# Four gate products behind the conformer, three steps of distance in the attention, and a projection tile behind each of ten chunks

## The chip, the cores and the metric

The kernel runs on one core of one Trainium2 chip. The metric is device microseconds of one execution, the median of several. The kernel before took 2198.22 us, the median of three runs from 2196.39 to 2204.89.

## The reference

Two layers of a hybrid trunk, over 1024 latent tokens and a context of 256, 1024 channels wide, in float32. The first layer adds a bidirectional state-space branch (SSD, 16 heads, chunks of 128 tokens: ten chunks with the context) and a conformer branch, whose result is multiplied by a gate; both go through one output projection. The second layer adds a gated chunk MLP and a windowed attention with sinks, again with one output projection.

```python
def even_mixer(h_x, h_c, w_in, ...):
    z_x, xbc_x, dt_x, glu_x, gate_x = _split(h_x @ w_in, EVEN_SIZES)
    ya_x, _, _ = ssd_branch(z_x, xbc_x, dt_x, hf_c, hb_c, ...)
    def merge(ya, glu, gate):
        yb = conformer_conv(glu, cv_w, cv_b, cv_ln_g, cv_ln_b) * jax.nn.silu(gate)
        return jnp.concatenate([ya, yb], axis=-1) @ w_out

def window_attention(q, k, v, k_ctx, v_ctx, sink):
    def block(args):
        s_lat = jnp.einsum('bqkrd,bskd->bkrqs', qblk, kblk) * ATT_SCALE
        s_lat = jnp.where(mblk, s_lat, -jnp.inf)
        s_ctx = jnp.einsum('bqkrd,bskd->bkrqs', qblk, k_ctx) * ATT_SCALE
        p = jax.nn.softmax(jnp.concatenate([s_lat, s_ctx, s_snk], axis=-1), axis=-1)
        return p[..., :3 * W] @ v_window + p[..., 3 * W:-1] @ v_ctx

def reference(x, c, ctx, c_ctx, ...):
    for layer in range(DEPTH):
        y_x, y_c = even_mixer(...) if layer % 2 == 0 else odd_mixer(...)
        x = layer_norm(DEEPNORM_ALPHA * x + g_x * y_x, ln_g[layer], ln_b[layer])
```

## The kernel before, in words

Every float32 product is made of three matmuls: each operand is split into a high part (a cast on ACT) and a low part (a subtraction on DVE or POOL), and high x high, low x high and high x low are summed in PSUM. So names come in pairs: hhi and hlo, wh and wl, zh and zl, yh and ylo, ph and pl.

**First layer, projections.** The input projection is computed channel by channel: 128 output channels over 1280 tokens in three slices (SLICES, two of 512 and one of 256 columns). The list `seq` sets the order of the GLU channels ("g"), the SSD channels ("x") and the early gates ("s"). An early gate's matmuls are followed by a SiLU on ACT and a store of the result to HBM (gs_d, L1277 and L1278), since its partner, the conformer's output cv, does not exist yet. After the list the conformer's layer norm is applied (it begins with the sums csum at L1324; its last scaling is L936 and L937), then z blocks 0 and 1 and early gate 2 are computed, then `dt_prep` (decays of the SSD on ACT and DVE, with small matmuls L1450 to L1492 and tables rA_d and rB_d stored at L1494), then `ssd_back`, the backward states of the ten chunks from the last to the first: each step loads a chunk (xtok, L1508), multiplies it on DVE (L1512), decays the state Hb on POOL (L1528), adds two bst matmuls (L1532, L1536) and stores the state to hb_d (L1523). z block 2 is computed beside it.

**Gates.** The loop at the end of `gates` takes the gates in the order 3, 0, 1, 4, 5, 6, 7, 2. `gate(i)` computes the first three with 75 matmuls each (L171) and multiplies the SiLU by cv[i] on POOL (L1393); for the five early ones it loads each slice of gs_d into one of four small tiles (tag "th"), multiplies it on POOL (L1386) and stores it to yb_d (L1387). Between them stand the loads of seven weight tiles wb of the output projection. yb_d is the input of the projection's second half.

**SSD stage and first output projection.** `stage_b(c)` is the part of the output projection that takes one chunk's 128 tokens of yb (48 matmuls at L1001; L159 splits its operands). It is written behind the SSD chunks: `S[c].prep`, `mix` and `finish` compute the forward states (tmp on POOL at L1567, two matmuls at L1574) and outputs. The order of instructions on each engine is set in this part of the program by the scheduler of the framework, which interleaves what is written; each engine then works in that order. SP issues nearly all DMAs, in order, and a DMA that waits holds those behind it.

**Attention.** It is the exception: the PE order is written by hand (L601). 16 units (4 key-value heads x 4 pairs of blocks) make 152 steps. A step computes the scores of one key block (L720, L721), takes the exponential (L723), splits it into ph (ACT, L730) and pl (POOL or DVE, L731), and LA steps later multiplies it with the values (L738). `att_max` is a generator that is advanced a few times in each step: it prepares the next unit's queries (mv, L664), makes score maxima (L678, L683), transposes the packed maxima (L705) and sends one row of them by POOL's DMA (L708) into the next unit's mv, which that unit's first L721 reads. `beside` fills each step with matmuls of `rest`: projections q and g, the opening of the second output projection ("W": gate rows by L222, weights wor loaded into the pool wr), its first half c (L1001) and its second half d (L832, with u from DVE at L842). What is left of `rest` when the last step is done runs as the tail.

```python
                LA = 2
                for n in range(len(seq) + LA):
...
                        fly.append(self.att_s(KV[kv % 2], mv[u], b, x, kb, off))
...
                now[0] = 99
                run(oth)
```

## Time and profile before

| | before |
|---|---|
| median of three runs | 2198.22 us |
| profiled execution | 2200.34 us, span 2198.6 us |
| PE matmul | 2054.9 us busy, 93% |
| DVE | 1348.8 us, 61% |
| ACT | 991.9 us, 45% |
| POOL | 979.8 us, 45% |
| mean granted clock of PE | 0.974 |
| chain that ended last | PE 64%, POOL 13%, DVE 9%, ACT 6%, DMA 5% |

Busy time of PE includes matmuls at a lower granted clock, so a stretch can be busy and still lose time. An engine other than PE matters where PE waits for it; the table of waits and the chain say where. The rows of single stages stand further below.

### The profile page before, as it was taken

Reading aid. Unit: us, or ns where it says so; the run is one execution under the profiler, and the core shown is the slowest. Engines: PE = TensorE matmul, PEld = TensorE weight load, DVE = VectorE, ACT = ScalarE, POOL = GpSimd, SP = SyncE. Lnnn points to the kernel's source line nnn. Section 1 sums busy time; section 2 is a strip of 40 time slices with the busy share of each in tenths; the row PEclk is TensorE's granted clock in tenths of the full one; section 3 lists DMA queues with packets and bytes.
Section 4 is the critical chain, followed back from the end, with each engine's and each line's share of the span. In section 5 each row is a group of like instructions: output and inputs, shape, how many; then the busy total and the mean of one; then the engine's idle time right before and its main releaser. Section 6 shows DMA issues by size and latency. Waiting matters only on the chain.

```text
span 2198.6 us, 28297 instructions
## 1 busy us (share of the span) xinstructions
PE 2054.9 (93%) x10636; PEld 1630.2 (74%) x10636; DVE 1348.8 (61%) x1889; ACT 991.9 (45%) x1549; POOL 979.8 (45%) x654
## 2 busy tenths in 40 slices
PE   7999999999979929999899999999999999899997
PEld 6888888889767716665488788888777676676675
DVE  6788896758445036667776321422566767676677
ACT  6455677533352122224234323233656767655510
POOL 0198999700112254546431113822445555434453
PEclk9999999999989969999899999999999999899998
DMA  8011122236637464464243422522311212534463
GB/s 306 30 39 39 51 79 85 96 129 213 218 106 250 169 221 149 146 214 157 98 159 125 134 70 82 179 99 80 99 49 51 59 52 57 159 92 126 122 182 130
DMA packets 158994, 269.33 MB, mean 123 GB/s; under 512 B 18901, under 2 KB 98385, under 8 KB 158601
## 3 DMA queue, kind: packets, MB, share of 16 engines
q1 hardware_dynamic: 157432, 264.01, 36.8%
q0 software_dynamic: 1280, 3.26, 0.5%
q8 instruction: 83, 1.36, 0.3%
q14 instruction: 55, 0.44, 0.1%
q10 hardware_dynamic: 144, 0.26, 0.0%
HBM read 189.82 MB, written 77.59 MB: 122 GB/s over the span
## 4 chain that ended last, share of the span: by engine, by line
PE 64%; POOL 13%; DVE 9%; ACT 6%; DMA 5%; issue 4%; SPq 0%; POOLq 0%; DVEq 0%; ACTq 0%
PE m L171 31%; PE m L1001 12%; POOL accq L1234 11%; PE po L738 3%; PE mz L1306 2%; PE po L1621 1%; PE m L832 1%; PE st L721 1%; PE st L720 1%; PE ms L208 1%; PE sg L1632 1%; ACT mv L664 1%; PE yd L1642 1%; ACT rb L425 1%; DVE wol L159 1%
## 5 line engine op out<-in xcount | busy, mean ns | idle before, releaser
L1234 POOL TENSOR_TENSOR accq<-accq,prod 128x1295 f32<-128x1295 f32 x90 | 287.7, 3197 | 33.9 <-ACT prod L1233 17.2
L171 PE MATMUL m<-hhi,wh 128*128 128x512 f32 (+1 forms) x792 | 280.9, 355 | 1.8 <-ACT th L1277 0.9
L171 PE MATMUL m<-hlo,wh 128*128 128x512 f32 (+1 forms) x792 | 280.6, 354 | 0.0
L171 PE MATMUL m<-hhi,wl 128*128 128x512 f32 (+1 forms) x792 | 280.2, 354 | 0.0
L1242 DVE SCALAR_TENSOR_TENSOR acc<-u,vwh,acc 128x1295 f32<-128x1295 f32 x150 | 235.2, 1568 | 12.9 <-ACT acc L1239 9.7
L731 POOL TENSOR_TENSOR pl<-pt,ph 128x512 fp32r<-128x512 f32 x96 | 130.1, 1356 | 198.9 <-ACT ph L730 195.9
L171 PE MATMUL m<-h1hi,wh 128*128 128x512 f32 (+1 forms) x544 | 213.3, 392 | 1.6 <-ACT rb L425 1.4
L171 PE MATMUL m<-h1lo,wh 128*128 128x512 f32 (+1 forms) x544 | 213.4, 392 | 0.0
L171 PE MATMUL m<-h1hi,wl 128*128 128x512 f32 (+1 forms) x544 | 212.3, 391 | 0.0
L1001 PE MATMUL m<-wol,yh 128*128 128x512 f32 x448 | 183.4, 409 | 4.6 <-DVE wol L954 2.5
L1001 PE MATMUL m<-woh,yh 128*128 128x512 f32 x448 | 185.9, 418 | 1.6 <-DVE t L1624 0.8
L1001 PE MATMUL m<-woh,ylo 128*128 128x512 f32 x448 | 181.6, 405 | 0.6 <-DVE ylo L159 0.6
L1233 ACT ACTIVATE prod<-u,vwh 128x1295 f32<-128x1295 f32 x90 | 124.1, 1382 | 97.9 <-POOL accq L1234 95.5
L171 PEld LDWEIGHTS m<-hhi,wh 128*128 128x128 f32 x792 | 149.7, 189 | 24.2 <-ACT th L1277 1.6
L171 PEld LDWEIGHTS m<-hhi,wl 128*128 128x128 f32 x792 | 149.7, 189 | 20.9
L171 PEld LDWEIGHTS m<-hlo,wh 128*128 128x128 f32 x792 | 149.8, 189 | 20.5
L730 ACT CAST ph<-pt 128x512 fp32r<-128x512 f32 x152 | 92.9, 619 | 97.6 <-PE po L738 86.2
L159 POOL TENSOR_TENSOR wl<-wr,wh 128x1024 fp32r<-128x1024 f32 x33 | 81.7, 2477 | 118.6 <-ACT wh L158 95.9
L738 PE MATMUL po<-ph,vs 128*66 128x512 f32 x304 | 121.6, 400 | 1.2 <-ACT ph L730 1.2
L171 PEld LDWEIGHTS m<-h1hi,wh 128*128 128x128 f32 x544 | 102.8, 189 | 22.6 <-ACT rb L425 2.0
L171 PEld LDWEIGHTS m<-h1hi,wl 128*128 128x128 f32 x544 | 102.9, 189 | 21.2
L171 PEld LDWEIGHTS m<-h1lo,wh 128*128 128x128 f32 x544 | 102.9, 189 | 19.9
(371 smaller groups left out, 4771.9 us busy)
## 6 DMA issues: line engine op xcount, KB each, us to landing
wr<-in_wch_dram SPq DMA_DIRECT2D x69, 512.0 KB
mw<-in_modw_dram SPq DMA_DIRECT2D x24, 512.0 KB
mr<-in_modw_dram SPq DMA_DIRECT2D x16, 512.0 KB
wor<-in_wout_dram SPq DMA_DIRECT2D x16, 512.0 KB
xbc_d<-acc SPq DMA_DIRECT2D x12, 640.0 KB
xcT<-xbc_d SPq DMA_DIRECT2D x20, 320.0 KB
xt_d<-xtok SPq DMA_DIRECT2D x20, 320.0 KB
xtok<-xt_d SPq DMA_DIRECT2D x10, 640.0 KB
```

The lines of the kernel that those rows point to most:

```text
L159: (nc.gpsimd if pool_lo else nc.vector).tensor_tensor(lo, src, hi.bitcast(F32), op=ALU.subtract)
L171: nc.tensor.matmul(out, x(k), y(k), start=(c == 0), stop=(c == tot - 1))
L208: nc.tensor.matmul(ps[:4, :P], self.scond[:, n * h + k], w[j][:, k], start=(h + j + k == 0), stop=(h + j + k == halves + n - 1))
L425: nc.scalar.copy(tb[d, :n], ps[s])
L730: nc.scalar.copy(ph, p)
L731: (nc.gpsimd if x in (0, 1, 3) else nc.vector).tensor_tensor(pl, p, ph.bitcast(F32), op=ALU.subtract)
L738: nc.tensor.matmul(po[:66], vs[:, kb, v], p[y], start=first and i == 0, stop=last and i == 2)
L1001: nc.tensor.matmul(ps[f], y[u][:, k], w[k][v][:, 512 * f:512 * f + 512], start=i + j == 0, stop=i + j == 9)
L1233: nc.scalar.activation(pr, u[:, k:k + N], AF.Copy, scale=vwh[:, i, k:k + 1])
L1234: nc.gpsimd.tensor_tensor(acc, acc, pr, op=ALU.add)
L1242: nc.vector.scalar_tensor_tensor(acc[:, :N], u[:, k:k + N], vwh[:, i, k:k + 1], acc[:, :N], op0=ALU.mult, op1=ALU.add)
L1306: nc.tensor.matmul(mz[0][32 * g:32 * g + 2, P * c:P * c + P], self.scond32[:, 2 * k:2 * k + 2], w[:, k], start=k == 0, stop=k == 7)
```

## The change

Four edits, made together.

- **Early products.** The gates 4 to 7 are still computed early. Directly behind the conformer, each of them is now loaded whole (128x1280) from gs_d into one tile gse (tag "accq", one buffer), multiplied by cv on POOL and stored to yb_d in three slices. Gate 2 is no longer an early gate: it is computed in the same place, but multiplied at once. The last loop holds the gates 3, 0 and 1 alone, with the weight loads in groups of three, two and two.
- **Projection tiles.** stage_b(2), with the operand y0, is written behind chunk 0 instead of ahead of the first chunk's prep, and a stage_b stands behind each of the ten chunks.
- **Attention.** LA is 3 instead of 2, ph and pl have three buffers instead of two, `att_max` yields four times instead of once behind mv, the opening of the second output projection (W) yields three times first, and the pool wr of its weights has two buffers instead of three, with two loaded ahead.
- **Tail.** The PSUM banks that the projection's halves take in turn are five instead of two once the last step of the attention is done.

```diff
--- before.py
+++ after.py
@@ -296,15 +296,13 @@
             self.mmt = ("m0", "m1")
             self.ko = (*range(1, 8), 0)
             S = [SsdFwd(self, c, xbc_d, xt_d, hb_d, zs_d, wt_d, rstd, q) for c in range(NT)]
-            self.stage_b(2, ob, w, yb_d, tb_d, grow, y0)
             S[0].prep()
             for c in range(NT):
                 S[c].mix()
                 if c < NT - 1:
                     S[c + 1].prep()
                 S[c].finish()
-                if c < NT - 1:
-                    self.stage_b((c + 3) % NT, ob, w, yb_d, tb_d, grow)
+                self.stage_b((c + 2) % NT, ob, w, yb_d, tb_d, grow, y0 if c == 0 else None)
                 if c == 7:
                     wl3 = ea.enter_context(self.pool(name="wl3", bufs=1))
                     for k in range(4, 6):
@@ -561,12 +559,14 @@
                         yield from (proj_q if n[0] == "q" else proj_g)(int(n[1]), int(n[2]))
                     elif n == "R":
                         self.er.close()
-                        wr = eq.enter_context(self.pool(name="wr", bufs=3))
+                        wr = eq.enter_context(self.pool(name="wr", bufs=2))
                         raws = []
-                        for k in range(3):
+                        for k in range(2):
                             raws.append(wr.tile([P, D], F32, name="wor", tag="wor"))
                             nc.sync.dma_start(raws[k], A["wout1"][k])
                     elif n == "W":
+                        for _ in range(3):
+                            yield None
                         ew.close()
                         free_h1()
                         out = self.out1_open(yc_d, wr, raws)
@@ -611,7 +611,7 @@
                 fly = []
                 mx = iter(())
                 acc = None
-                LA = 2
+                LA = 3
                 for n in range(len(seq) + LA):
                     if n < len(seq):
                         u, b, x, kb, off = seq[n]
@@ -647,6 +647,7 @@
                     beside(d * 0.2)
                     next(mx, None)
                 now[0] = 99
+                self.mmt = ("m0", "m1", "m2", "ms", "ms")
                 run(oth)
             eq.close()
 
@@ -665,7 +666,8 @@
                 nc.vector.tensor_tensor(mv2[0:64, :, 2 * i + hh], src,
                                         mv1[64 * hh:64 * hh + 64, :, 2 * i + hh].bitcast(F32), op=ALU.subtract)
         out[u] = mv1, mv2
-        yield
+        for _ in range(4):
+            yield
         pack_ = q.tile([P, 2, 2, 4], F32, name="mpack")
         mx = q.tile([P, 2, 2, 4], F32, name="mxs")
         for b in range(2):
@@ -725,8 +727,8 @@
 
             nc.gpsimd.affine_select(out=p, in_=p, pattern=[[0, 4], [off, P]], base=0, channel_multiplier=-off,
                                     compare_op=ALU.is_ge, fill=0.0)
-        ph = q.tile([P, 4, P], FR, name="ph", bufs=2)
-        pl = q.tile([P, 4, P], FR, name="pl", bufs=2)
+        ph = q.tile([P, 4, P], FR, name="ph", bufs=3)
+        pl = q.tile([P, 4, P], FR, name="pl", bufs=3)
         nc.scalar.copy(ph, p)
         (nc.gpsimd if x in (0, 1, 3) else nc.vector).tensor_tensor(pl, p, ph.bitcast(F32), op=ALU.subtract)
         return ph, pl
@@ -1267,7 +1269,7 @@
 
         order = [0, 1, 2, 3, 4, 5, 6, 7]
         seq = "gggggggxsxsxsxsxxxxxxxxg"
-        early = (4, 5, 6, 7, 2)
+        early = (4, 5, 6, 7)
         g = x = ge = 0
 
         def gate_early(i):
@@ -1323,6 +1325,13 @@
         for i in order[2:]:
             nc.gpsimd.tensor_tensor(csum[:, :T], csum[:, :T], cv[i][:, :T], op=ALU.add)
         self.conformer(cv, csum, ecf)
+
+        for i in early:
+            gt = aq.tile([P, 1295], F32, name="gse", tag="accq")
+            nc.sync.dma_start(gt[:, :T], gs_d[i])
+            nc.gpsimd.tensor_tensor(gt[:, :T], cv[i][:, :T], gt[:, :T], op=ALU.mult)
+            for a, b in SLICES:
+                nc.sync.dma_start(yb_d[a][i], gt[:, a:b])
 
         def token_major(xq, c, h):
 
@@ -1369,8 +1378,17 @@
                             nc.sync.dma_start(zs_d[t, :, 352 * j - 32:352 * j + 320], zs[:, :352])
                 assert not xq or not todo
 
+        def gate(i):
+            def ev(ps, a, b):
+                gt = tq.tile([P, 512], F32, name="gs", tag="th")
+                nc.scalar.activation(gt[:, :b - a], ps, AF.Silu)
+                nc.gpsimd.tensor_tensor(gt[:, :b - a], cv[i][:, a:b], gt[:, :b - a], op=ALU.mult)
+                nc.sync.dma_start(yb_d[a][i], gt[:, :b - a])
+
+            self.proj_ch(wp, W[28 + i], hhi, hlo, ev)
+
         zblocks((0, 1))
-        gate_early(2)
+        gate(2)
         ecf.close()
         self.s0 = s0.__enter__()
         self.dt_prep(dtr)
@@ -1378,30 +1396,15 @@
         zblocks((2,))
         em.close()
 
-        def gate(i):
-            if i in early:
-                for a, b in SLICES:
-                    gt = tq.tile([P, 512], F32, name="gs", tag="th")
-                    nc.sync.dma_start(gt[:, :b - a], gs_d[i, :, a:b])
-                    nc.gpsimd.tensor_tensor(gt[:, :b - a], cv[i][:, a:b], gt[:, :b - a], op=ALU.mult)
-                    nc.sync.dma_start(yb_d[a][i], gt[:, :b - a])
-                return
-
-            def ev(ps, a, b):
-                gt = tq.tile([P, 512], F32, name="gs", tag="th")
-                nc.scalar.activation(gt[:, :b - a], ps, AF.Silu)
-                nc.gpsimd.tensor_tensor(gt[:, :b - a], cv[i][:, a:b], gt[:, :b - a], op=ALU.mult)
-                nc.sync.dma_start(yb_d[a][i], gt[:, :b - a])
-
-            self.proj_ch(wp, W[28 + i], hhi, hlo, ev)
-
         ewl = self.ewl = ExitStack()
         wl = ewl.enter_context(self.pool(name="wl", bufs=1, side="right"))
         wb = [(k, wl.tile([P, D], F32, name=f"wb{k}", tag=f"wb{k}"), (wl, f"wb{k}")) for k in range(1, 8)]
-        for n, i in enumerate((3, 0, 1, 4, 5, 6, 7, 2)):
+        k = 0
+        for i, m in ((3, 3), (0, 5), (1, 7)):
             gate(i)
-            if n:
-                nc.sync.dma_start(wb[n - 1][1], A["wout0"][8 + n])
+            for k in range(k, m):
+                nc.sync.dma_start(wb[k][1], A["wout0"][9 + k])
+            k = m
         we = ewl.enter_context(self.pool(name="we", bufs=1, side="right"))
         y = wl.tile([P, 8, P], F32, name="yl0", tag="wb0")
         nc.sync.dma_start(y, yb_d[256][:, :, :P].rearrange("k p t -> p k t"))
```

The lines of the changed kernel lie two or three higher than those of the kernel before (L1508 becomes L1511, L1001 becomes L1003, L1574 becomes L1577).

The order of the instructions shows what the scheduler makes of it. First SP's queue, from the end of the conformer to the first stores of the backward state. Before (rA_d and rB_d are dt_prep's tables, xtok the loads of the chunks, wr the weights of z and of the gates, Hb the backward state):

```order
L1494 DMA rA_d<-rt 96x10x128
L1494 DMA rB_d<-rt 96x10x128
L1508 DMA xtok<-xt_d 128x1280 x2
L1150 DMA wr<-in_wzdt_dram 128x704 x2
L1150 DMA wr<-in_wch_dram 128x1024 x2
L1508 DMA xtok<-xt_d 128x1280
L1523 DMA hb_d<-Hb 128x1024
```

And in the changed kernel (gse are the early products, here from the load of the third on):

```order
L1497 DMA rA_d<-rt 96x10x128
L1331 DMA gse<-gs_d 128x1280
L1497 DMA rB_d<-rt 96x10x128
L1334 DMA yb_d<-gse 128x512 x2
L1334 DMA yb_d<-gse 128x256
L1511 DMA xtok<-xt_d 128x1280 x2
L1331 DMA gse<-gs_d 128x1280
L1511 DMA xtok<-xt_d 128x1280
L1526 DMA hb_d<-Hb 128x1024
```

The first chunk loads stand behind the third product's stores and the third behind the fourth product's load; the weights of z (wzdt), directly behind the first chunk loads before, follow further down, behind two stores of the state.

Second PE, behind the last matmuls of dt_prep (L1492, L1495 now) and the gate rows (L222). Before:

```order
L1492 MATMUL ms<-cs,xparts 96x128 x20
L222 MATMUL ms<-cs,gcol 128x128 x8
L171 MATMUL m_5830<-zh,hhi 128x352
L171 MATMUL m_5868<-zh,hhi 128x352
L171 MATMUL m_5906<-zh,hhi 128x352
L171 MATMUL m_5830<-zl,hhi 128x352
```

And in the changed kernel, where L1535 is the backward state's matmul:

```order
L1495 MATMUL ms<-cs,xparts 96x128 x20
L222 MATMUL ms<-cs,gcol 128x128 x8
L1535 MATMUL bst<-xtok 128x512 x6
L171 MATMUL m_5857<-zh,hhi 128x352
L171 MATMUL m_5895<-zh,hhi 128x352
L171 MATMUL m_5933<-zh,hhi 128x352
```

Six matmuls of the backward state, three steps of it, moved ahead of z block 2 (zh, zl).

Third PE at the end of the gates' matmuls (L171), where the SSD stage and the first output projection begin. Before:

```order
L171 MATMUL m_6422<-hhi,wl 128x256
L222 MATMUL ms<-cs,gcol 128x128 x8
L1574 MATMUL ms<-tmp,xt_6684 128x512 x2
L1001 MATMUL m_6627<-woh_6549,yh_6522 128x512
L1001 MATMUL m_6628<-woh_6549,yh_6522 128x512
L1001 MATMUL m_6627<-wol_6550,yh_6522 128x512
```

And in the changed kernel:

```order
L171 MATMUL m_6453<-hhi,wl 128x256
L222 MATMUL ms<-cs,gcol 128x128 x8
L1003 MATMUL m_6769<-woh_6516,yh_6489 128x512
L1003 MATMUL m_6770<-woh_6516,yh_6489 128x512
L1003 MATMUL m_6769<-wol_6517,yh_6489 128x512
```

The first chunk's state (L1574 before, reading POOL's tmp) stood ahead of the projection's first matmul; in the changed kernel 44 matmuls of the projection stand ahead of it.

## Rows read from the trace of the kernel before

**Rows 1.** Windows of the first layer's end, core 0; columns in the first row.

```profile
core 0: us, PE busy (x) PEld busy (x) DVE busy (x) ACT busy (x) POOL busy (x), PEclk, DMA share, GB/s
643.00:664.00 21.00, 9.02 (x43) 6.76 (x41) 7.26 (x16) 11.15 (x19) 0.00 (x0) 0.59 0.15 37
664.00:721.00 57.00, 55.16 (x283) 45.35 (x282) 32.82 (x51) 8.91 (x14) 15.70 (x9) 1.00 0.76 262
...
764.00:807.00 43.00, 2.05 (x16) 1.86 (x16) 1.65 (x1) 11.73 (x15) 19.88 (x19) 0.56 0.83 269
807.00:1042.00 235.00, 228.71 (x1237) 146.23 (x1238) 168.31 (x225) 66.17 (x94) 128.16 (x77) 0.99 0.49 163
1042.00:1088.00 46.00, 36.28 (x235) 17.84 (x231) 33.75 (x53) 12.54 (x21) 24.49 (x19) 0.81 0.30 103
```

**Rows 2.** Chain of waits, 760 to 830 us: start, us, what.

```profile
765.47 4.68 DMA gs<-gs_d
...
771.26 4.25 DMA yb_d<-gs
```

**Rows 3.** Timeline of PE, 788 to 812 us: start, us, engine, line, [idle before].

```profile
807.02 3.57 PE L1574 MATMUL ms<-tmp,xt 128*128 128x512 f32 x4 [40.40 <-POOL tmp L1567]
...
809.81 1.25 PE L1001 MATMUL m<-woh,yh 128*128 128x512 f32 x2
```

**Rows 4.** Two lines: count, ns min/median/max, first and last start.

```profile
L1324 POOL TENSOR_TENSOR csum<-csum,u x6: 2946/2958/3837, 410.7 to 545.4; 128x1280 f32<-128x1280 f32 x6
...
L1536 DVE TENSOR_TENSOR Hb<-Hb,bst x16: 673/680/689, 681.4 to 720.8; 128x512 f32<-128x512 f32 x16
```

**Rows 5.** Timeline around two loads of a chunk, SP, DVE and POOL.

```profile
682.40 0.42 SPq L1508 DMA_DIRECT2D xtok<-xt_d  x1
...
687.65 1.23 DVE L1512 TENSOR_TENSOR xtok<-xtok,wst 128x1024 f32<-128x1024 f32 x1 [2.55 <-DMA xtok<-xt_d]
...
696.67 1.90 POOL L1528 TENSOR_TENSOR Hb<-Hb,expS 128x1024 f32<-128x1024 f32 x1 [4.44 <-DVE Hb L1536]
...
696.80 2.85 DVE L1512 TENSOR_TENSOR xtok<-xtok,wst 128x1024 f32<-128x1024 f32 x1 [0.26 <-DMA xtok<-xt_d]
```

**Rows 6.** Timeline of ACT, 634 to 645 us: the conformer's last scaling.

```profile
638.59 4.04 ACT L937 ACTIVATE u<-u,vecs 128x256 f32<-128x256 f32 x8 [3.13 <-DVE u L936]
```

**Rows 7.** Chain of waits, 640 to 764 us.

```profile
665.16 7.09 DMA wr<-in_wzdt_dram
...
685.35 0.86 PE bst L1532 x2
...
720.75 42.82 PE m L171 x225
```

**Rows 8.** Waits of PE in the attention and after it, 1592 to 2199 us.

```profile
PE po L738 <- DVE pl L731: 9.3, 6, 4.0
...
PE m L222 <- DVE gdt L525: 5.0, 1, 5.0
PE ms L678 <- ACT mv L664: 4.9, 8, 1.1
PE po L738 <- POOL pl L731: 3.5, 3, 1.7
```

**Rows 9.** Timeline around one unit's maxima, 2044 to 2053 us.

```profile
2044.29 0.28 PE L705 MATMUL ms<-cs,mpack 128*16 128x128 f32 x1
...
2052.48 0.40 PE L721 MATMUL st<-mv,ks 65*128 65x512 f32 x1
...
2045.58 0.55 POOL L708 DMA_DIRECT2D mv<-prow  x1
...
DMA to landing us min/median/max: 1.6/1.6/4.4
```

**Rows 10.** Timeline of PE after the longest wait of the tail.

```profile
2153.65 0.77 PE L832 MATMUL m<-woh,yh 128*128 128x512 f32 x1 [4.44 <-DVE u L842]
...
2158.74 0.39 PE L832 MATMUL m<-woh,yh 128*128 128x512 f32 x1
```

## Prediction

> **What bounds the kernel now.** I read the busy shares first: TensorE's matmuls fill 93% of the span, so time can only go where PE stands still or runs at its lower clock. The windows of the first layer's end show where that is [rows 1]. From 807 to 1042 us PE is busy 228.71 of 235 us, so that stage is bound by PE itself. The three stretches around it are not: 643 to 664 us (9.02 of 21, granted clock 0.59), 764 to 807 us (2.05 of 43, clock 0.56), 1042 to 1088 us (36.28 of 46, clock 0.81). The chain of waits tells what the second one consists of: the early gates' slices come back from HBM, are multiplied on POOL and stored again, one behind the other through four small tiles, with a load piece of 4.68 and a store piece of 4.25 us standing in the chain [rows 2]. PE waits 40.40 us in one piece, at line 1574, for the POOL product that stands behind them, and begins the output projection at 809.81 us [rows 3].
>
> **Part 1, the early products behind the conformer.** The 43 us stretch loses its reason. But the products don't vanish: four of 128x1280 now run through one single tile, each load, product, store in sequence, because the next load waits until the stores have read the tile. The order shows what stands behind them. On SP the loads of the SSD chunks (xtok) now stand behind the stores of the third product; on POOL the decay of the backward state (L1528) stands behind all four; on PE three backward steps (bst x6) now stand ahead of z block 2, and PE takes no matmul of z while they wait. The second step's PSUM tiles come free only when that decay and two DVE additions are done, so PE reaches z behind product four.
>
> One cycle, from rows: a product of the same shape is L1324, 2.95 to 3.84 us [rows 4]. A load of the same 640 KB took 5.25 us from its issue to its reader [rows 5]; the short end is the 4.68 us of [rows 2], and the store is bounded by 4.25 there and by 5.25. The cycle is then 4.68 + 2.95 + 4.25 = 11.9 to 5.25 + 3.84 + 5.25 = 14.3 us; I take the middle, 13.1. The first product starts when the conformer's last slice is done, 638.59 + 4.04 = 642.6 us [rows 6], and ends at 646.0 with the middle value, 3.4. The fourth ends three cycles later, 685.3. The decay, 1.90 [rows 5], two DVE additions of 0.68 [rows 4] and a pair of bst matmuls of 0.86 [rows 7] bring z to 689.4 us; with the ends of the cycle 685 to 694. Before, it began as the second window opens, at 664: 25 us later. From this comes off what z no longer holds: three steps of two pairs, 6 x 0.86 = 5.2 us. On top comes a wait for the second pieces of z's weights, which now stand behind two stores of the backward state: a load of them took 7.09 us [rows 7], so 0 to 7; I take half, 3.5. Gates 3, 0 and 1 follow with their 42.82 us (from 720.75, [rows 7]). They end at 763.6 + 25.4 - 5.2 + 3.5 = 787 us.
>
> The output projection's first tile (y0) is loaded behind the first slice of gate 1, so what follows the gates is short: 5 us (2 to 8) for the last preparation, against 46 before. PE resumes at 792 instead of 809.81, a lead of 18, of which 2.8 go to the L1574 group that stood ahead before (807.02 to 809.81, [rows 3]) and is still to do. Some of the lead is lost because the projection's matmuls, PE's filler for the SSD chunks, are used up slightly earlier, while the last stretch [rows 1] has none left in either order. **Term 1: -14 us**, ends -8 and -22.
>
> Work that I cost at nothing: gate 2's product, now made at once on POOL. A slice of 512 columns is two fifths of a product of 1280, 1.2 to 1.5 us by [rows 4], and two stand ahead of the conformer's last scale. The gate is done well ahead of it, which hides them; without that cover z is 2.4 to 3 us later. The grouped loads of the projection's weights lie beside 43 us of gates.
>
> **Part 2, the projection's tile behind each of the ten chunks.** The first tile's 48 matmuls are the same; the scheduler puts the tile first in both kernels. What is gained, PE not waiting for POOL at L1574, is in term 1. **Term 2: 0**, with an end of +-3 us: the 2.8 of the L1574 group.
>
> **Part 3, the distances in the attention.** PE waits there for the low part of the probabilities, pl, 9.3 + 3.5 us [rows 8]. A third step between scores and their use gives each of these nine waits a step more, about 2.8 us, and only the longest, 4.0, can keep 1.2 of it. The 1.7 on POOL lies at the opening of the second output projection, where there is little other work; so 12.8 - 1.2 - 1.7 = 10 are free to go. The next operand may be late instead, so I take 9. Four yields instead of one behind the copies take the wait on mv, 4.9 in 8 pieces [rows 8]: 4. Against it: the maxima's transpose (L705) comes one step later. In the unit shown it is at 2044.29, its row is sent at 2045.58 and lands 1.6 us after, and the next unit reads it at 2052.48, three steps on [rows 9]: 8.2 us, of which 5.4 are left, for a need of 2.9. The longest send of the sixteen took 4.4 instead of 1.6, so one or two may wait: +1. At the opening of the second output projection three yields give its gate rows the 5.0 us that PE now waits for [rows 8], but only two of its weight tiles are loaded ahead instead of three, and a later load of about 5 us may not be covered: -5 to +5, taken as -1. **Term 3: -13 us**, ends -4 and -20.
>
> **Part 4, five PSUM banks in the tail.** With two banks PE stops for DVE's reading of the one before, 4.44 us in the longest piece [rows 10]. Behind it the clock is down, and 12 matmuls take from 2153.65 to 2158.74, 5.1 us; the gates' 225 matmuls, two of 512 columns to each of 256, took 42.82 [rows 7], which is 0.23 for one of 512, or 2.7 for 12. So 4.4 + 2.4 = 6.8 is the most that this piece gives. DVE's own work and the load of the next token tile are late next. **Term 4: -6 us**, ends -3 and -7.
>
> Sum: -14 - 13 - 6 = -33 us against the profiled execution's 2200.34, of which 2198.6 is span. The median is 2.1 below it: 2198.22 - 33 = 2165 us. All ends together: -8 - 4 - 3 + 3 = -12 to -22 - 20 - 7 - 3 = -52, or 2146 to 2186.
>
> **One rule against one row.** DVE's multiplication of a chunk took 1.23 us at 687.65 and 2.85 at 696.80, and the second began 0.13 us after a POOL product (L1528) of 1.90 us [rows 5]. The product's 3.84 against 2.95 [rows 4] is like it on the other side. So DVE and POOL hold one another, and in 643 to 664 us, where POOL did nothing, there now are products. The Trainium skill ("SBUF — State Buffer", Who interferes with whom) says that a DVE instruction with two SBUF inputs contends with a GpSimd instruction that reads SBUF, and that one of them blocks fully; the trace agrees. By that rule the worst price of these rows would be the usual one, and the time 2170 us; by their middle values the sum stays at 2165. This is rival C.
>
> **The rivals.**
> A, the forecast: 2165 us, chance 0.52.
> B, the early products hold SP and POOL longer. The stores and loads meet the other transfers (DMA is 0.76 busy in 664 to 721, [rows 1]), and the cycle is 18 us instead of 13.1. Three cycles later by 4.9 each: 14.7 us, and term 1 is about 0. 2165 + 14 = 2179 us, chance 0.15. For it: chunk loads and stores join the products' on one queue; against it: the DMA share ahead of 664 us is 0.15.
> C, DVE and POOL hold each other: the four products take 3.84 each, 4 x 0.4 = 1.8 over the 3.4 of the sum, and the first two chunk multiplications are 2.85 - 1.23 = 1.6 longer each, 3.2. Together 5 us: 2170 us, chance 0.10. The dt chain itself, also longer by up to two products, stays hidden behind the fourth product.
> D, the waits in the attention only change their place: PE stalls at the next operand and term 3 is 0. 2178 us, chance 0.14. For it: the same order of DVE's and POOL's work makes pl late; against it: the waits are nine pieces in 152 steps, not one in each.
> E, slower: the row of the maxima comes late for the next unit. Mechanism: L705 is 2.8 us later in the unit, its send stands in POOL's order behind one probability subtraction more (1.2 to 1.5 us, two fifths of [rows 4]), and PE, in order, waits at L721. It decides from the point where the row lands later than 5.4 us behind L705 [rows 9]. If each send is as slow as the slowest, the row lands 2.9 + 2.8 + 1.5 = 7.2 us behind it, 1.8 late; the clock that falls behind a wait adds up to the tail's 2.4 [rows 10], taken as 1.6. In 15 units this is 15 x 3.4 = 51 us: 2165 + 51 = 2216 us, chance 0.09. Against it: in the shown unit 2 us are to spare.
>
> **How the numbers follow.** 0.5%, 11 us, is about what a measurement of this kernel can tell from no change: the bounds are 2187 and 2209 us. A and C are faster wholly (0.62), B and D in three quarters (0.22): faster 0.84. A quarter of B and D (0.07) and a fifth of E (0.02) lie within: same 0.09. Slower 0.07. The range takes in nearly all ends of the forecast, and B and D with some 11 us that they may lose besides: 2148 to 2190; left out are E and the outer parts of B and D.
>
> **What would show it.** Right: z block 2's first matmul at 685 to 694 us, behind six bst matmuls; gates 3, 0, 1 end at 782 to 792; the next matmul within 8 us, with no wait at the L1574 group; PE's waits on pl and ph in the attention below 4 us in all, mv gone; no wait of 4 us at L832 in the tail. Wrong: z later than 697 (B); the products at 3.8 us and dt steps of 2 to 3 us (C); waits at L721 in many units (E); waits for pl as many as before (D).

## The result, and the profile after

| | before | changed |
|---|---|---|
| median | 2198.99 us (four runs, 2196.39 to 2204.89) | 2161.04 us (four runs, 2159.51 to 2163.65) |
| ratio, 95% interval | | 0.9827, 0.9814 to 0.984 |
| span of the profiled execution | 2198.6 us | 2157.5 us |
| PE matmul busy | 2054.9 us, 93% | 2050.3 us, 95% |
| mean granted clock | 0.974 | 0.980 |

The kernel is 38 us faster, where 33 were forecast. PE's work is the same; 36 us of the 41 by which the span is shorter are time in which it stood still. Where they come from is read from marks in the two traces, each but the last the start of a matmul:

| mark, us | before | changed | difference |
|---|---|---|---|
| first GLU matmul with a low weight (jitter ahead of the change) | 84.1 | 82.6 | -1.5 |
| last matmul of the gates (L171) | 763.3 | 785.0 | +21.7 |
| first of the first output projection | 809.8 | 788.6 | -21.2 |
| last of the SSD stage | 1093.8 | 1064.3 | -29.5 |
| first score | 1606.7 | 1575.8 | -30.9 |
| last score | 2079.7 | 2037.6 | -42.1 |
| end | 2198.6 | 2157.5 | -41.1 |

So in these two profiles the end of the first layer gave 28 us after the jitter and the attention 11; the tail gave nothing, it is 1 us longer.

The windows of the same stretches as [rows 1], of the changed kernel (window, length, busy us and count of PE, weight loads, DVE, ACT and POOL, granted clock, DMA share, GB/s):

```profile
643.00:664.00 21.00, 6.72 (x36) 4.77 (x35) 10.50 (x17) 8.32 (x14) 3.80 (x2) 0.66 0.41 126
664.00:721.00 57.00, 41.78 (x179) 30.23 (x178) 29.51 (x42) 9.51 (x14) 18.15 (x9) 0.82 0.76 255
...
764.00:807.00 43.00, 40.23 (x202) 32.84 (x201) 15.70 (x15) 14.52 (x20) 15.21 (x10) 1.00 0.47 150
...
1042.00:1088.00 46.00, 41.64 (x229) 30.25 (x229) 31.64 (x45) 13.30 (x20) 18.23 (x16) 0.95 0.40 133
```

The stretch from 764 to 807 us is full (40.23 of 43 us, before 2.05). What was paid for it stands ahead: PE is busy 6.72 us of 21 and 41.78 of 57, at granted clocks of 0.66 and 0.82, where [rows 1] have 9.02 and 55.16. The last stretch, with 36.28 us of 46 before, has 41.64.

The four early products on POOL, from its timeline (start, us, engine, line, tile, idle before and its reason):

```profile
641.03 2.89 POOL L1332 TENSOR_TENSOR gse<-u,gse 128x1280 f32<-128x1280 f32 x1 [0.25 <-ACT u L939]
651.18 2.88 POOL L1332 TENSOR_TENSOR gse<-u,gse 128x1280 f32<-128x1280 f32 x1 [7.26 <-DMA gse<-gs_d]
666.78 2.88 POOL L1332 TENSOR_TENSOR gse<-u,gse 128x1280 f32<-128x1280 f32 x1 [12.72 <-DMA gse<-gs_d]
678.86 2.89 POOL L1332 TENSOR_TENSOR gse<-u,gse 128x1280 f32<-128x1280 f32 x1 [9.20 <-DMA gse<-gs_d]
```

Each takes 2.88 or 2.89 us, none the 3.84 of [rows 4]. They begin 10.2, 15.6 and 12.1 us apart. The second gap is the long one. SP's queue shows why:

```profile
647.09 0.32 SPq L1331 DMA_DIRECT2D gse<-gs_d  x1
...
654.09 1.28 SPq L1334 DMA_DIRECT2D yb_d<-gse  x3
660.01 0.33 SPq L1497 DMA_DIRECT2D rA_d<-rt  x1
660.45 0.49 SPq L1331 DMA_DIRECT2D gse<-gs_d  x1
...
671.08 0.89 SPq L1511 DMA_DIRECT2D xtok<-xt_d  x2
```

The second load of gse (647.09) stands behind nothing but the first product's stores. The second product's stores are out at 655.4. The table rA_d stands next in the queue and waits until 660.01 for the dt chain (the steps of dt_prep that make the table). Only then can the third load of gse be issued, and behind the third product's stores the first chunk loads, at 671.08.

PE in the same time, and at the start of the projection:

```profile
676.42 5.97 PE L1535 MATMUL bst<-xtok 128*128 128x512 f32 x8 [7.96 <-DVE xtok L1515]
687.30 3.78 PE L1535 MATMUL bst<-xtok 128*128 128x512 f32 x4 [4.91 <-DVE Hb L1539]
690.09 1.61 PE L171 MATMUL m<-zh,hhi 128*128 128x352 f32 x3
...
788.58 0.71 PE L1003 MATMUL m<-woh,yh 128*128 128x512 f32 x2
```

PE waits 7.96 us for the first chunk and 4.91 for the second step's addition, and begins z block 2 (z from here on) at 690.09. The projection begins at 788.58, 21.2 us ahead of [rows 3].

Two rows of DVE before, which were not shown ahead, and then the same two instructions in the changed kernel, with the decay on POOL behind the fourth product and the third chunk's multiplication on DVE:

```profile
640.79 2.06 DVE L1435 SCALAR_TENSOR_TENSOR pp__5589<-pp__5589,z 128x320 f32<-128x320 f32 x4
...
649.09 0.49 DVE L1471 TENSOR_TENSOR wst<-tmpS,dtd 128x320 f32<-128x320 f32 x1 [0.54 <-ACT tmpS L1465]
```

```profile
640.59 4.73 DVE L1438 SCALAR_TENSOR_TENSOR pp__5616<-pp__5616,z 128x320 f32<-128x320 f32 x4
...
651.55 2.86 DVE L1474 TENSOR_TENSOR wst<-tmpS,dtd 128x320 f32<-128x320 f32 x1 [0.54 <-ACT tmpS L1468]
...
681.72 1.90 POOL L1531 TENSOR_TENSOR Hb<-Hb,expS 128x1024 f32<-128x1024 f32 x1
...
685.42 1.23 DVE L1515 TENSOR_TENSOR xtok<-xtok,wst 128x1024 f32<-128x1024 f32 x1 [4.49 <-DMA xtok<-xt_d]
```

Beside the first product four polynomial steps take 4.73 us instead of 2.06, and beside the second the 0.49 us step takes 2.86. The dt chain ends some 4 us later: rA_d went out at 655.93 before and goes out at 660.01. The last two rows show what was last for z: the fourth product ended at 681.75 and the decay at 683.62, but the third chunk, issued at 680.23, reached DVE at 685.42, and the second step's addition stands behind its multiplication on DVE. A second path ends close to it: ACT makes zh, which z reads, only from 688.35 on, and by the profile it waited for the fourth product's stores.

PE's waits in the attention (1570 to 2060 us; total, times, longest), which answer to [rows 8]:

```profile
PE po L740 <- DVE pl L733: 4.2, 3, 3.8
PE po L740 <- ACT yo L745: 3.8, 6, 0.9
PE m L222 <- DVE gdt L523: 3.6, 1, 3.6
PE st L723 <- DMA mv<-prow: 3.3, 2, 2.1
```

The waits for pl fell from 12.8 to 4.2 us and those for mv are gone. Of the 4.2, one piece of 3.8 lies behind the last score, as one of 4.0 did before. New are 3.3 us for the row of the maxima, in two units, and 3.8 for the accumulator's copy yo; the gate rows still wait 3.6 us. From the last score to the end (2037 to 2158 us):

```profile
PE po L740 <- DVE pl L733: 3.8, 1, 3.8
PE m L834 <- DVE ylo L159: 3.3, 1, 3.3
PE m L834 <- ACT yh L158: 3.2, 1, 3.2
```

No wait for a bank of the projection's second half (u L842, [rows 10]) is left; one of 2.4 us for a bank of the first half (u L773) stands in both kernels. PE waits for its operands ylo and yh instead, and the wait of 3.8 for pl is the one named above. SP's queue in the tail:

```profile
2107.27 0.36 SPq L851 DMA_DIRECT2D out_dram<-xl  x1
...
2113.14 0.33 SPq L867 DMA_DIRECT2D xl<-tc_d  x1
2113.56 0.38 SPq L812 DMA_DIRECT2D ks<-gd_d  x1
```

An output store is issued at 2107.27. The next residual tile is to go into the same buffer, and its load waits for that store until 2113.14; the operand load behind it (ks) is held with it.

### The profile page after: what moved, and what is told of

Read it like the earlier page. It is cut to its first block, busy times and chain, and to the rows that moved or that the text cites. A ratio compares the mean times of both kernels' runs of the same rounds, so it can differ in the third digit from the quotient of the medians.

```text
span 2157.5 us, 28255 instructions
## 1 busy us (share of the span) xinstructions
PE 2050.3 (95%) x10636; PEld 1631.5 (76%) x10636; DVE 1344.7 (62%) x1889; ACT 990.9 (46%) x1549; POOL 980.0 (45%) x646
## 5 line engine op out<-in xcount | busy, mean ns | idle before, releaser
L171 PE MATMUL m<-hhi,wh 128*128 128x512 f32 (+1 forms) x792 | 280.9, 355 | 1.8 <-ACT th L1279 0.9
L171 PE MATMUL m<-hlo,wh 128*128 128x512 f32 (+1 forms) x792 | 280.6, 354 | 0.0
L171 PE MATMUL m<-hhi,wl 128*128 128x512 f32 (+1 forms) x792 | 280.2, 354 | 0.0
L171 PE MATMUL m<-h1hi,wh 128*128 128x512 f32 (+1 forms) x544 | 213.2, 392 | 1.7 <-ACT rb L423 1.4
L171 PE MATMUL m<-h1lo,wh 128*128 128x512 f32 (+1 forms) x544 | 213.0, 392 | 0.0
L171 PE MATMUL m<-h1hi,wl 128*128 128x512 f32 (+1 forms) x544 | 212.1, 390 | 0.0
L1003 PE MATMUL m<-wol,yh 128*128 128x512 f32 x448 | 182.1, 406 | 1.3 <-DVE wol L956 1.1
L1003 PE MATMUL m<-woh,yh 128*128 128x512 f32 x448 | 181.4, 408 | 1.8 <-ACT yh L158 0.9
L1003 PE MATMUL m<-woh,ylo 128*128 128x512 f32 x448 | 182.0, 406 | 0.3 <-DVE ylo L159 0.3
L171 PEld LDWEIGHTS m<-hhi,wh 128*128 128x128 f32 x792 | 149.7, 189 | 24.1 <-ACT th L1279 1.6
L171 PEld LDWEIGHTS m<-hhi,wl 128*128 128x128 f32 x792 | 149.7, 189 | 20.8
L171 PEld LDWEIGHTS m<-hlo,wh 128*128 128x128 f32 x792 | 149.8, 189 | 20.6
L171 PEld LDWEIGHTS m<-h1hi,wh 128*128 128x128 f32 x544 | 102.7, 189 | 22.9 <-ACT rb L423 2.0
L171 PEld LDWEIGHTS m<-h1hi,wl 128*128 128x128 f32 x544 | 102.6, 189 | 21.0 <-issue 0.2
L171 PEld LDWEIGHTS m<-h1lo,wh 128*128 128x128 f32 x544 | 102.8, 189 | 19.7
```

What stands on the lines that cost most here:

```text
L171: nc.tensor.matmul(out, x(k), y(k), start=(c == 0), stop=(c == tot - 1))
L1003: nc.tensor.matmul(ps[f], y[u][:, k], w[k][v][:, 512 * f:512 * f + 512], start=i + j == 0, stop=i + j == 9)
```

## The experiments

Each stretch below is read from the profiled execution of its kernel, and kernels with the same code in a stretch give the spread to keep in mind. From first to last score it is 470.9 to 473.0 us in the four kernels with the attention of before, and 461.8 to 465.2 in the seven with the changed one. The SSD stage (from the start of the projection to the mark of the table) takes 281.7 to 288.0 us in the five kernels with the first layer of before, and 274.4 to 275.9 in the five with the early products and the gates in the changed kernel's order. From the last score to the end it is 118.4 to 121.1 us in the three with attention and tail of before, and 119.3 to 121.4 in the three with both as changed. Each ratio is to the kernel before.

**The four parts alone.** First the early products:

```diff
-        early = (4, 5, 6, 7, 2)
+        early = (4, 5, 6, 7)
...
+        for i in early:
+            gt = aq.tile([P, 1295], F32, name="gse", tag="accq")
+            nc.sync.dma_start(gt[:, :T], gs_d[i])
+            nc.gpsimd.tensor_tensor(gt[:, :T], cv[i][:, :T], gt[:, :T], op=ALU.mult)
+            for a, b in SLICES:
+                nc.sync.dma_start(yb_d[a][i], gt[:, a:b])
...
-        for n, i in enumerate((3, 0, 1, 4, 5, 6, 7, 2)):
+        for i, m in ((3, 3), (0, 5), (1, 7)):
```

> The kernel before with the early products alone (gates 4 to 7 behind the conformer, gate 2 multiplied at once, three gates in the last loop). Theory 1: the whole gain ahead of the second layer, some 28 us of the two profiles, is this part's: the 43 us stretch goes (some 20 us after the later start of z) and PE's start on the projection ahead of the first chunk's state gives the other 8. Expected -25 to -31 us. Rival: those 8 us come from where the projection's tiles are written (part B), then this kernel shows -17 to -22 us and b_only -6 to -10.

Measured: 2170.18 us, ratio 0.9854 (0.9831 to 0.9877). The last gate ends at 787.2, the projection begins at 791.2, the SSD stage takes 275.4 us as in the whole change (275.7). The median is 31 us below the kernel before, at the end of what was expected. So the whole gain of the first layer is this part's, the shorter SSD stage included.

Then the projection's tiles:

```diff
-            self.stage_b(2, ob, w, yb_d, tb_d, grow, y0)
             S[0].prep()
...
-                if c < NT - 1:
-                    self.stage_b((c + 3) % NT, ob, w, yb_d, tb_d, grow)
+                self.stage_b((c + 2) % NT, ob, w, yb_d, tb_d, grow, y0 if c == 0 else None)
```

> The kernel before with stage_b(2) behind chunk 0 and a tile behind each of the ten chunks alone. Theory 1: within 2 us of before, since L1574 still stands ahead of the projection on PE and waits for POOL as before. Rival: -6 to -10 us, a better spread of the projection's matmuls over the chunks.

Measured: 2195.89 us, ratio 0.9979 (0.9965 to 0.9993), some 5 us faster, between the two expectations. Its SSD stage took 280.1 us, 1.6 below the shortest of the five without it, so where the rest comes from stays open. Behind the early products nothing of it is seen, since the stage is as long with it as without.

The attention without the five banks:

```diff
-                        wr = eq.enter_context(self.pool(name="wr", bufs=3))
+                        wr = eq.enter_context(self.pool(name="wr", bufs=2))
...
+                        for _ in range(3):
+                            yield None
                         ew.close()
...
-                LA = 2
+                LA = 3
...
-        yield
+        for _ in range(4):
+            yield
...
```

> The kernel before with the attention's distances alone (LA 3, three buffers of ph and pl, four yields behind mv, three ahead of W, two weight buffers), without the five banks. Theory 1: -9 to -12 us, all between the first and the last score, new waits on the row of the maxima near 3 us and on the buffer of the closed accumulator near 4 us. Rival: some of it belongs to the later phase in which the attention meets the transfers, then it is under 6 us.

Measured: 2193.3 us, ratio 0.9959 (0.9945 to 0.9972), some 9 us; 463.6 us from first to last score. Its waits:

```profile
PE st L724 <- DMA mv<-prow: 3.9, 2, 2.2
PE po L741 <- ACT yo L746: 3.8, 6, 1.0
...
PE po L741 <- DVE pl L734: 2.4, 2, 2.2
```

The row costs 3.9 us in two units, yo 3.8, as expected, and pl is down to 2.4.

The five banks:

```diff
                 now[0] = 99
+                self.mmt = ("m0", "m1", "m2", "ms", "ms")
                 run(oth)
```

> The kernel before with five PSUM banks in the tail alone. My forecast's step: -6 us (-3 to -7). Theory after the profile of the change: 0, within 2 us, since the tail is bound by the loop of output store, load of the next token tile and DVE, and PE waits for the tile's operands (ylo, yh) in place of the bank.

Measured: 2201.14 us, ratio 1.0001 (0.9989 to 1.0013). PE's waits in its tail:

```profile
PE m L833 <- ACT yh L158: 2.6, 1, 2.6
PE m L833 <- DVE ylo L159: 2.5, 1, 2.5
```

5.1 us for the operands have taken the place of the 5.8 for u, and the stretch from the last score to the end is 119.7 us, inside the spread: the banks gave nothing. The four ratios multiply to 0.979, the whole is 0.983; with the intervals of the parts, up to 0.0023 to either side, that is no clear difference.

**What holds the tail.** Two residual tiles in a tile that the attention no longer needs, in place of the two buffers that take turns:

```diff
-        x = ob.tile([P, D], F32, name="xl", tag="xl")
+        x = q.tile([P, D], F32, name="mv1", tag="mv1") if t in (4, 5) else ob.tile([P, D], F32, name="xl", tag="xl")
```

> The changed kernel with the residual tiles of the tail's token tiles 4 and 5 taken from a dead tile of the attention (mv1), so that their loads don't wait until an output store has read the buffer. Theory: the tail is bound by that loop, in which the waiting load also holds the operand loads behind it on SP's queue; with it gone, the stretch from the last score to the end falls from 120 us by 4 to 8, and PE's waits for ylo and yh (6.5 us) mostly go; time near 2154. Rival: the operands themselves (gate and denominator loads, POOL's products) bound the tail, then it stays within 2 us of the change, 2161.

Measured: 2157.89 us, ratio 0.9814 (0.9793 to 0.9834); the tail took 115.7 us, 4.2 less than in the changed kernel, the low end of what was expected. The longest of its waits for operands:

```profile
PE m L834 <- ACT yh L158: 2.7, 2, 2.4
```

The operands' waits fell from 7.3 to 4.1 us (one of 0.8 in each kernel and two of 0.3 here are not shown), and the last two residual tiles are loaded at 2116.68 and 2117.89, where the changed kernel loads them at 2128.29 and 2136.86. The two later kernels with the same edit (v_all and v_g30, below) have tails of 116.5 and 114.8 us, so all three lie below the 119.3 to 121.4 of the changed tail. So a part of the tail is that loop and its hold on SP; the intervals of the two ratios overlap, so as a gain in the median it is not shown.

**Whether the dt chain is on the path to z.**

```diff
-                nc.sync.dma_start(dst.rearrange("d c t h l -> (d c t h) l").rearrange("(j p) l -> p j l", p=96), rt)
+                nc.scalar.dma_start(dst.rearrange("d c t h l -> (d c t h) l").rearrange("(j p) l -> p j l", p=96), rt)
```

> The changed kernel with dt_prep's two tables stored by ACT's queue instead of SP's. Theory: in the changed kernel the first table's store, which waits for the dt chain until 660.0, holds the load of the third product by some 3 us, so the dt chain, lengthened beside the products by DVE waiting for POOL, is on the path to z; here the third load is issued near 657 and z begins 2 to 4 us earlier (686 to 688 instead of 690). Rival, as in my forecast: the dt chain stays hidden behind the products and z begins at 690 within 1 us.

```profile
646.25 1.30 SPq L1334 DMA_DIRECT2D yb_d<-gse  x3
...
656.40 1.29 SPq L1334 DMA_DIRECT2D yb_d<-gse  x3
659.60 0.32 SPq L1331 DMA_DIRECT2D gse<-gs_d  x1
...
686.65 1.57 PE L171 MATMUL m<-zh,hhi 128*128 128x352 f32 x3
```

Measured: 2156.61 us, ratio 0.9798 (0.9771 to 0.9826). The third load goes out at 659.60, 1.9 us behind the second product's stores, and z begins at 686.65. This execution had its first product 2.3 us later than the changed kernel's; from that product's first store to z it is 40.4 us against 46.1, and 45.8 to 46.6 in the other three kernels with that queue. So the tables' place in SP's queue was on the path: 5.7 us to z, more than the 2 to 4 expected, and the rival is out. In the median the gain is not shown, since the two intervals overlap.

**Whether PE's empty time ahead of z can be filled.**

```diff
         gate(2)
+        gate(3)
         ecf.close()
...
-        for i, m in ((3, 3), (0, 5), (1, 7)):
+        for i, m in ((0, 3), (1, 7)):
```

> The changed kernel with gate 3 computed directly behind gate 2, ahead of dt_prep, instead of behind z block 2. Theory: PE stands still for most of 643 to 690 us because the products and the chunk loads behind them set the start of z; 14.3 us of matmuls fit there, z begins 0 to 6 us later and the last gate ends 8 to 14 us earlier: 2147 to 2153 us. Rival: gate 3 delays the dt chain and the products behind it by its whole length, then z begins 14 us later and the time is within 2 us of the change.

The changed kernel's window from 643 to 690 us, then this kernel's:

```profile
643.00:690.00 47.00, 19.70 (x68) 11.51 (x67) 17.59 (x25) 11.25 (x19) 13.33 (x6) 0.65 0.59 195
```

```profile
643.00:690.00 47.00, 29.86 (x153) 20.56 (x152) 14.55 (x29) 14.59 (x27) 16.24 (x9) 0.78 0.64 217
```

And this kernel's first matmuls of z and of the projection, from PE's timeline:

```profile
695.48 0.75 PE L171 MATMUL m<-zh,hhi 128*128 128x352 f32 x3
...
776.83 0.71 PE L1003 MATMUL m<-woh,yh 128*128 128x512 f32 x2
```

Measured: 2147.86 us, ratio 0.9758 (0.9737 to 0.9778), clear of the changed kernel's interval. PE is busy 29.86 us of the 47 instead of 19.70, z begins 5.4 us later, and the projection 11.8 us earlier, as the theory had it.

**Together.** The three edits in one kernel:

```diff
+        gate(3)
...
+                nc.scalar.dma_start(dst.rearrange("d c t h l -> (d c t h) l").rearrange("(j p) l -> p j l", p=96), rt)
...
+        x = q.tile([P, D], F32, name="mv1", tag="mv1") if t in (4, 5) else ob.tile([P, D], F32, name="xl", tag="xl")
```

> The changed kernel with three of the edits tried together: gate 3 behind gate 2, the two tables on ACT's queue, the tail's tiles 4 and 5 in dead tiles. Theory: gate 3 took 13 us, the tail 4, and of the tables' 5 about half is left since gate 3 already fills that time: 2140 to 2146 us. Rival: the three work on the same slack and it stays at 2147 to 2150, as with gate 3 alone.

Measured: 2145.7 us, ratio 0.9753 (0.973 to 0.9777): the lowest of all, just inside the expected 2140 to 2146, but not to be told from gate 3 alone, so between theory and rival nothing is settled. In its profile, the slowest of its four executions, the tail's part is there (116.5 us), but the SSD stage took 280.2 us where gate 3 alone has 273.4; why is open. And with gate 0 as well:

```diff
+        gate(3)
+        gate(0)
...
-        for i, m in ((0, 3), (1, 7)):
+        for i, m in ((1, 7),):
```

> As v_all with gate 0 too behind gate 2 and 3, ahead of dt_prep. Theory: between 650 and 690 us some 20 us of PE's time are still empty behind gate 3, but the dt chain (20 us from its first matmul to the gate rows) now starts 14 us later and comes on the path: gain 0 to 6 us over v_all. Rival: the products and chunk loads still set z's start, then the whole 14 us are gained: near 2130.

Measured: 2149.43 us, ratio 0.9767 (0.9749 to 0.9785). The last gate ended at 764.5, but the projection began at 774.3, 10 us behind it, and nothing was gained over v_all:

```profile
774.29 1.22 PE L1003 MATMUL m<-woh,yh 128*128 128x512 f32 x2 [6.48 <-ACT yh L158]
```

PE waits 6.48 us for the projection's first operand. In SP's queue the loads of all seven weight tiles now go out from 750.87 on, ahead of the last gate's stores and of the operand's load at 764.41, and DMA is 0.96 busy in these 10 us. That these transfers are the new limit is read from the trace; no run tried it.

**The attention's parts.** The third step of distance alone (with the room that it needs):

```diff
-                        wr = eq.enter_context(self.pool(name="wr", bufs=3))
+                        wr = eq.enter_context(self.pool(name="wr", bufs=2))
...
-                LA = 2
+                LA = 3
...
```

> The kernel before with the third step of distance alone (LA 3, three buffers of ph and pl, two weight buffers, which the room asks for), no yields added. Theory: the waits for pl and ph (14 us before) fall to under 3, the waits on mv (5) stay, and the stretch from first to last score falls from 473 to 464 to 467: -6 to -9 us. Rival: half the attention's gain was the yields', then 468 to 471.

Measured: 2205.14 us, ratio 1.0018 (1.0002 to 1.0033). 473.3 us from first to last score, 0.3 more than before. Its waits:

```profile
PE m L832 <- DVE u L842: 9.6, 4, 4.0
PE ms L678 <- ACT mv L664: 6.2, 9, 1.1
...
PE m L683 <- DVE mxs L690: 3.1, 7, 0.7
```

The waits for pl are gone wholly, as expected, but the time is not: PE now waits for the maxima's own operands, mv (6.2 us) and mxs (8.0 in all forms, of which the largest is shown), and for u in the tail. The four yields alone:

```diff
         out[u] = mv1, mv2
-        yield
+        for _ in range(4):
+            yield
```

> The kernel before with four yields behind mv alone. Theory: mv's waits (5 us) go, the row's late landing costs 1 to 4, the stretch from first to last score falls by 1 to 4 from 473. Rival: the whole maxima come a step later and PE waits for them, stretch 473 to 477, slower.

Measured: 2208.76 us, ratio 1.0043 (1.003 to 1.0056): slower, and beyond both expectations. 491.1 us from first to last score:

```profile
PE m L833 <- DVE u L843: 11.4, 5, 4.5
PE st L722 <- DMA mv<-prow: 7.7, 6, 2.7
PE po L739 <- ACT yo L744: 7.1, 4, 2.4
...
PE po L739 <- DVE pl L732: 5.0, 5, 2.3
```

The row of the maxima is late in six units, 7.7 us, yo costs 7.1, and pl still waits, 7.2 us with the two pieces on POOL that are not shown. Half the yields in the changed kernel:

```diff
-        for _ in range(4):
+        for _ in range(2):
             yield
```

> The changed kernel with two yields behind mv in the maxima instead of four. Theory: the four yields took the waits on mv (5 us before) but made the row of the maxima late in two units (3.3 us, its first wait); with two, the row's wait is under 1 us and mv's under 2, and the stretch from first to last score stays 462 within 2 us. Rival: the waits on the row come from somewhat slow sends and stay.

Measured: 2168.42 us, ratio 0.9858 (0.9837 to 0.9878), slower than the change. The stretch from first to last score is 459.2 us, 2.6 shorter than in the changed kernel, which is no more than its spread; the row's wait is gone and mv's is 2.0, about as expected. But the tail is 7.6 us longer:

```profile
PE m L834 <- DVE u L773: 7.8, 1, 7.8
...
PE ms L680 <- ACT mv L665: 2.0, 4, 0.7
```

PE waits 7.8 us in one piece for u (L773) of the projection's first half as the attention ends, where it was 2.4: the bank that DVE must read is late. Seven matmuls of the first half (L1003) now lie behind the last score, where the changed kernel has none, so its last bank comes to DVE later; that this is the whole of the 7.8 us was not tried.

## Why the prediction was right, and where its steps failed

The time, the sign and the mechanism of the largest term held; the sizes of three terms did not, and that they made up for one another is luck. Of the forecast's signs for being right, z, the end of the gates and the start of the projection came; the waits on pl are 4.2 us instead of below 4, and the wait at the L1574 group is 1.0 us instead of none.

**Term 1 (-14, ends -8 and -22): 28 us after the jitter, beyond the far end.** The chain was right in its marks: z at 690.1 for 689.4, the last gate's end at 785 for 787, the projection at 788.6 for 792. The 3.5 us for z's second weights were not there: from z to the end of the gates it is 94.9 us against 99.1, and PE's one wait in z is 1.9 us for ACT. The mis-sized piece is what became of the lead. I took 4 of the 18 us off, for L1574's group and for the projection's matmuls that run out; instead the SSD stage was 8.3 us shorter. a_only shows that this belongs to the early products, and the spread of the two groups (274.4 to 275.9 against 281.7 to 288.0) that it is no accident of one execution. PE stood still 10.3 us in the stage instead of 16.0, with less waiting for DVE; why was not tried, and it stays open.

**Within term 1, one step failed though its number came out.** "The dt chain ... stays hidden behind the fourth product": DVE's steps beside the products were held as rival C says, the chain became 4 us longer, and its table stood ahead of the third product's load on SP. v_rab shows 5.7 us. That it came out near 690 is luck: the first product began 1.6 us earlier than in the sum, and the cycles were 10.2, 15.6 and 12.1 us instead of 13.1. A cycle in which nothing else stands in the queue took 10.2: 2.88 for the product instead of 3.4, 3.2 from its end to the next load (643.92 to 647.09) instead of 4.75, and 4.1 from there to the next product instead of 5. The end of the chain was also another: from the fourth product's end to z it was 8.3 us instead of 4.1, of which 3.7 went until the third chunk had come (the sum had 1.9 for the decay), 1.9 on its multiplication and an addition on DVE, and 2.8 on the third step's matmuls, at a granted clock of 0.50.

**Term 2 (0, +-3): -5 alone, and 0 beside the early products.** By the median, the end of 3 was too narrow for the part alone; in the change, whose SSD stage is as long without it, the value holds.

**Term 3 (-13): -11 from first to last score.** That is the far end of the spread: between the two groups of kernels it is 6 to 11 us, and c_only gave 9. So the size lies inside the ends of -4 and -20, but the sum that made it is wrong. Taken apart, the distance gave 0 in that stretch and the yields +18, and both kernels were slower, by 0.2 and 0.4%; with the yields ahead of W they gave 9. The yields ahead of W were not run without the others, so what makes the three together pay is not shown. A wait that goes only shows the next operand in the same step, and two edits that each move a waiting operand are not two terms. That was rival D's mechanism, which each part alone shows. Rival E's is in c_y as well: six units wait for the row, but 1.3 us each, not 3.4.

**Term 4 (-6): +1, which is 0 within the spread.** I had named DVE's work and the next tile's load as late next and still kept 6 of the 6.8. t_only shows 0 in the time, with the operands' wait in the bank's place; v_x3 that the loop of store, load and SP's queue holds part of it.

**Rivals B and C.** The cycle was 12.6 on average, not 18. Of C, the half on DVE came, with steps of 3 us that were its sign; POOL was not held in the four products, which took 2.88 or 2.89.

## What to carry to other kernels

Work taken out of a serial stretch at the end of a phase and put where an engine is idle paid here although the new place makes the next phase start 26 us later. Where the engine that bounds the kernel then stands still, as between 643 and 690 us, look for work that depends on neither: one gate of 14 us moved there gave another 13. On an in-order queue read what each waiting DMA holds behind it, a store of a table as much as a load. Before adding up the waits that an edit removes, ask of each step which operand is second: an experiment with each part alone tells whether the sum is one.

## What the runs showed of the hardware

In the places looked at, where a DVE step with both inputs in SBUF meets a POOL product, the one that comes later takes longer by nearly as much as the earlier one has left. DVE came later beside the first two early products: the step of 0.49 us that began at 651.55, 0.37 us after a product, ended at 654.41, 0.35 us after the product, which took its usual 2.88. The third and fourth product had no such step beside them. Further on in the same trace POOL came later:

```profile
691.75 0.88 DVE L159 TENSOR_TENSOR zl<-wr,zh 128x704 fp32r<-128x704 f32 x1
...
691.95 2.44 POOL L1531 TENSOR_TENSOR Hb<-Hb,expS 128x1024 f32<-128x1024 f32 x1 [2.08 <-DVE Hb L1539]
```

The decay, 1.90 us at 681.72, took 2.44 behind a DVE step that had begun 0.20 us before it and had 0.68 left. The Trainium skill ("SBUF — State Buffer", Who interferes with whom) says that a DVE instruction with two SBUF inputs contends with a GpSimd instruction that reads SBUF, and that issue order decides who blocks; the trace agrees.

How long a load waits for the stores out of its tile is not one figure. In v_rab it went out 1.9 us after the last store's issue (657.69 to 659.60, DMA 0.57 busy); in the tail of the changed kernel it was 5.5 us (2107.63 to 2113.14, DMA 0.71 busy), and a store piece of the last loop took 4.25 us [rows 2]. What sets it was not tried.
